# Four cosine channels in one stacked product, and PSUM pools divided at two stage starts, in a hybrid Fourier and convolution block

## The chip, the core and the metric

The kernel runs on one core of one Trainium2 chip. The metric is the device time of one execution in microseconds (us); of several executions the median counts. Times inside a run are read from one execution that the hardware profiler recorded, and are counted from the start of its span.

## What is computed

One encoder block over 1040 positions (16 meta tokens and 1024 inputs) of width 1024, all in float32. Cut to what matters here:

```
h     = rmsnorm(h_res)
u_a, c_g, b_g, v_b, gate_logits = split(h @ w_in)
y_a   = fourier_mix(u_a) @ w_fourier          # real part of fft2 over positions and the
                                              # 128 channels of each of 4 groups
y_b   = (b_g * dwconv(c_g * v_b)) @ w_conv_out
g0,g1 = sigmoid(gate_logits + b_gates)
h_res = h_res + rmsnorm((g0 * y_a + g1 * y_b) @ w_out)
up    = dwconv(rmsnorm(h_res) @ w_up);  a, v = split(up)
out   = h_res + rmsnorm((gelu(a) * v) @ w_down)
```

## The kernel before

**Products.** Each float32 operand is split into a high and a low part (`split`, lines 127 and 128: ACT casts the high part, DVE subtracts it to get the low one), and each product is made of three matmuls (`mm3`, lines 159, 161, 163: high x high, low x high, high x low). The large projections go through pairs of blocks with seven products each; the accumulators of such a pair are called a, b, c, d, of 514 or 512 columns each, and `B_c` and `up_c` are the last to be computed of the last pair before the Fourier stage and before the down projection. DVE (`B_s`, `up_1x`, line 144) adds them to others when PE has finished them.

**Fourier stage.** The real part of the 2-D transform needs, by symmetry, 65 cosine and 63 sine channels of each group of 128. `transformed` multiplies w_u by the channel transform while the projections run, and two ACT copies (line 612) put its result in the order: 260 cosine columns (4 groups of 65), then 252 sine columns (4 groups of 63). `fold` folds the positions, and both go to DRAM (`fold_d`). `next_fold(kt)` loads one of eight pieces `u` back (777 KB), and splits it. `u_mm(kt)` (line 731) makes 30 matmuls per kt, for five row blocks i of 105 or 101 positions, into five accumulators `pq0` to `pq4`. When kt = 7 is done, the accumulators are split into `pqh` and `pql`, and `dft` multiplies them by tables of cosines and sines (`cosh`, `cosl`, `sinh`, `sinl`, split from `cosr` and `sinr`, which are loaded inside this stage behind the splits of u4 and u5, whose memory they take over).

The cosine channels, 260 of them, are handled as three tiles `MA` of 87, 87 and 86 rows, the sine channels, 252, as two tiles `MB` of 126. `dft` writes them transposed and split: `ath`, `atl`, `bth`, `btl`.

**Merge.** For each of eight column blocks f of 128: `merge_operands(f)` loads the Fourier weights (`wfa`, `wfb`: the rows of channel k and of its mirror, which DVE adds or subtracts), the convolution weights and the gates. PE makes `yp` (cosine part: three tiles x three matmuls x two position chunks of 262 and 260 columns = 18 matmuls), `yq` (sine part, 12), and `yb` (convolution part, 36). DVE combines them: `y` from yp and yq, `s <- s, y`, then `s <- yb, s`. From f = 5 on, `out_weights` also loads and splits a block of w_out (`wor`, `wo`). `project(0)` follows.

**Later.** The gated MLP's up projection runs in pairs, and the down projection (products `dna` and `dnb` of 12 matmuls per k, operands `gd` and `wd`) in seven steps over 11 k.

**What sets the order.** Each engine runs its own list of instructions in order; the list follows the program with moves by a scheduler, and waits are by semaphore on what an instruction depends on. SP issues nearly all DMAs, in order. In PSUM there are eight banks. Each stage opens a pool of eight banks, and tiles get banks in the order of allocation; a tile waits until the last reader of the tile that had its bank is done. In before, `pq0` gets bank 0, that of `B_c`'s first half, and the first of `dna` bank 0, that of `up_c`.

Of the kernel before, what the change touches and what calls it, by code (L numbers as in the profile page):

```python
# [24 lines left out]
G = 4  # L25
# [25 lines left out]
HP = H + 1  # L51
Q = L // 4 + 1
NCH = [(0, 262), (262, 260)]
LT = 105
NLT = 5
# [4 lines left out]
FW = 2 * H  # L60
KC, KS = 65, 63
NA, NB = G * KC, G * KS
MA = [(0, 87), (87, 87), (174, 86)]
MB = [(0, 126), (126, 126)]


# [18 lines left out]

@with_exitstack
def block_kernel(ctx, tc, xT, w_u, w_in, w_fa, w_fa2, w_fb, w_fb2, w_co, w_out, w_up, w_dn,
                 par, dch, cos_t, sin_t, outT):
# [30 lines left out]
    V, S, SP = nc.vector, nc.scalar, nc.sync  # L119
# [4 lines left out]
    def split(hi, lo, src, scale=None, eng=V, copy=S.copy):  # L124

        if scale is None:
            a = copy(hi, src)  # L127
            b = eng.tensor_tensor(out=lo, in0=src, in1=hi.bitcast(F32), op=ALU.subtract)
# [14 lines left out]
    def add(out, a, b, eng=V):  # L143
        return eng.tensor_tensor(out=out, in0=a, in1=b, op=ALU.add).ins  # L144
# [101 lines left out]
    ring = Ring()  # L246
# [355 lines left out]
    def transformed(kt):  # L602

        r = ring.raw(f"wu{kt}")
        SP.dma_start(r[:, :512], w_u[kt])
        wp = wtile(psum, f"wp{kt}")[:, :512]
        for g in range(G):
            nc.tensor.matmul(wp[:, g * P : (g + 1) * P], r[:, g * P : (g + 1) * P], dc, start=True, stop=True)
        src = wp.rearrange("p (g k) -> p g k", k=P)
        t = r[:, 512:]  # L610
        for s, at, k in ((src[:, :, :KC], slice(0, NA), KC), (src[:, :, KC:], slice(NA, 512), KS)):
            S.copy(t[:, at].rearrange("p (g k) -> p g k", k=k), s)
        SP.dma_start(fold_d[kt, :, FW:], t)

    def fold(kt):
# [45 lines left out]


    mix_s = ExitStack()
    psum_s, psum = scope("psum2", 8, space=PSUM)

    COS_ROOMS = ("t2h", "t2l")
    SIN_ROOMS = ("t3h", "t4h")
# [7 lines left out]
    def merge_operands(f):  # L675
        s = room(S_ROOMS[f % 3], F32, f"s{f}")
        s0, s1 = s[:, :NT], s[:, NT : 2 * NT]
        ra, rb = ring.raw(f"wfa{f}"), ring.raw(f"wfb{f}")
        SP.dma_start(ra[:87, :384], w_fa[f])
        SP.dma_start(ra[:87, 384:768], w_fa2[f])  # L680
# [5 lines left out]
        add(ra[:87, :384], ra[:87, :384], ra[:87, 384:768])  # L686
        sub(rb[:126, :256], rb[:126, 256:512], rb[:126, :256])
        into = [None] * 3
        if f == 0:
            a, b = room("t1l", F32R, "w0a"), room("t4l", F32R, "w0b")  # L690
            into = [(a[:, :384], a[:, 384:768]), (a[:, 768:1024], a[:, 1024:1280]), (b[:, :512], b[:, 512:1024])]
        return s0, s1, [
            ring.piece(f"w{i}_{f}", src, p, t)
            for i, src, p, t in zip("abc", (ra[:87, :384], rb[:126, :256], rb[:, 512:]), (87, 126, P), into)
        ]

    def gated_conv():
# [9 lines left out]
            parts.append((hi, lo))  # L707
        return list(zip(*parts))

    def bank(name):  # L710
        return psum.tile([P, 512], F32, tag="bank", name=name)

    tp_ = new_pool(mix_s, "trans")
    ath, atl = (tp_.tile([P, 3, HP], F32R, name=n) for n in ("ath", "atl"))
    bth, btl = (tp_.tile([P, 2, HP], F32R, name=n) for n in ("bth", "btl"))

    with ExitStack() as st:
        fp = new_pool(st, "four", side="right")
        pqh, pql = (fp.tile([P, NLT, 512], F32R, name=n) for n in ("pqh", "pql"))
        acc = [bank(f"pq{i}") for i in range(NLT)]  # L720

        def u_mm(kt, xs, wc):
            (ch, cl), (sh, sl) = xs
            wh, wl = wc
            for i in range(NLT):
                n, s = _lrows(i), slice(i * LT, i * LT + _lrows(i))
                oa, ob = acc[i][:n, :NA], acc[i][:n, NA:]

                for o, (xh, xl), ks in ((oa, (ch, cl), slice(0, NA)), (ob, (sh, sl), slice(NA, 512))):
                    for n_, (a, b) in enumerate(((xh, wh), (xh, wl), (xl, wh))):  # L730
                        nc.tensor.matmul(  # L731
                            o, a[:, s], b[:, ks], start=kt == n_ == ks.start == 0, stop=kt == KT - 1 and n_ == 2,
                            skip_group_check=True,
                        )

        def table(tab, name, at):
            raw = room(at, F32, f"{name}r")[:LT, :TW]
            return raw, SP.dma_start(raw, tab).ins

        def table_parts(raw, name, at):  # L740
            parts = [room(n, F32R, f"{name}{i}")[:LT, :TW] for n, i in zip(at, "hl")]
            split(*parts, raw)
            return parts

        next_fold(4)
        for kt in range(KT):
            u_mm(kt, *folded[kt])
            if kt + 5 < KT:
                next_fold(kt + 5)
            if kt == 2:  # L750
                cos_r, _ = table(cos_t, "cos", "b11h")
                sin_r, last = table(sin_t, "sin", "t1l")
        cos_p = table_parts(cos_r, "cos", COS_ROOMS)
        sin_p = table_parts(sin_r, "sin", SIN_ROOMS)
        for i in range(NLT):
            n = _lrows(i)
            done = split(pqh[:n, i, :], pql[:n, i, :], acc[i][:n, :])

        def dft(tab, x, y, ms):
            (xh, xl), (yh, yl) = x, y  # L760
            name = f"dft{len(ms)}"
            at = 0
            for c, (a, w) in enumerate(NCH):
                outs = [bank(f"{name}_{m}_{c}") for m in range(len(ms))]
                for i in KINDS[c]:
                    n = _lrows(i)
                    th, tl = (t[:n, at : at + w] for t in tab)
                    at += w
                    for m, (m0, mw) in enumerate(ms):
                        mm3(  # L770
                            [outs[m][:mw, :w]],
                            (xh[:n, i, m0 : m0 + mw], xl[:n, i, m0 : m0 + mw]),
                            ([th], [tl]),
                            i == KINDS[c][0],
                            i == KINDS[c][-1],
                        )
                for m, (_, mw) in enumerate(ms):
                    split(yh[:mw, m, a : a + w], yl[:mw, m, a : a + w], outs[m][:mw, :w])

        dft(cos_p, (pqh[:, :, :NA], pql[:, :, :NA]), (ath, atl), MA)  # L780
        with behind(last, *done):
            merge_ins = [merge_operands(0)]
            ybs = gated_conv()
        dft(sin_p, (pqh[:, :, NA:], pql[:, :, NA:]), (bth, btl), MB)
    keep_s.close()
    ring.open(mix_s, "mergew", 7)
    op = new_pool(out_s, "proj", side="right")
# [17 lines left out]
    m0 = []  # L805
    for f in range(KT):
# [6 lines left out]
        yp = [bank(f"yp{f}_{c}") for c in range(2)]  # L813
        yq = [bank(f"yq{f}_{c}") for c in range(2)]
        for ps, w, (zh, zl), ms in ((yp, wa, (ath, atl), MA), (yq, wb, (bth, btl), MB)):
            for m, (_, mw) in enumerate(ms):
                mm3(
                    [o[:, :n] for o, (_, n) in zip(ps, NCH)],
                    tuple(t[:mw, m * P : (m + 1) * P] for t in w),
                    ([zh[:mw, m, a : a + n] for a, n in NCH], [zl[:mw, m, a : a + n] for a, n in NCH]),  # L820
                    m == 0,
                    m == len(ms) - 1,
                )
        for c, (a, n) in enumerate(NCH):
# [421 lines left out]

    dn_s, psum = scope("psum5", 8, space=PSUM)
    fn = new_pool(dn_s, "fin")  # L1250
    places = [f"{n}{i}" for n in ("b11", "t4", "t2", "t3", "b21", "b22", "t1") for i in "hl"]
    pairs_ = [r[:, i * 1024 : (i + 1) * 1024] for r in (room(t, F32, f"wd_{t}") for t in places[:NK]) for i in range(2)]
# [246 lines left out]
```

## Time and profile before

| | us |
|---|---|
| Median of 3 runs | 1219.29 |
| Lowest and highest | 1216.8, 1221.27 |
| The profiled execution | 1222.5 |
| Its span | 1220.7 |
| PE busy in the span | 1186.2 (97%) |
| DVE busy | 1001.6 (82%) |
| ACT busy | 550.6 (45%) |
| POOL busy | 0.4 (6 instructions) |
| TensorE clock, mean | 0.986 of full |

The stages by the trace: the projections up to 312.7; the Fourier stage's `pq` 314.85 to 345.1 and `dft` up to 356.1; the merge up to about 432; then w_out, the norms, and the up projection up to 989.0; the down projection from 991.9. In a row of the timeline stand the start, the time, the engine, the line, the operation, output and inputs, the shape, and in brackets how long the engine had been idle before and what it waited for. "x2" sums up two instructions. A row of the windows gives a stretch, the busy time of PE, PEld, DVE, ACT and POOL with the count of instructions, the clock granted to TensorE, the DMA engines' busy share and GB/s.

### The profile page before, as it was taken

What the parts mean: (1) busy time and instruction counts of PE and PEld (TensorE: products, weight loads), DVE (VectorE), ACT (ScalarE), POOL (GpSimd) and SP (SyncE); (2) the same over time, 40 slices, a digit from 0 to 9 for tenths busy, and PEclk for the clock granted to TensorE, in tenths of its full rate; (3) what the DMA queues carried; (4) which work ended last, traced back from release to release, by engine and by line L of the source; (5) the groups of instructions that cost most, each with busy time, mean ns of one, the idle gap of its engine ahead of it and who ended that gap; (6) DMA issues with size and microseconds to landing.
All of it is one profiled execution on the core that took longest, in us unless ns stands there. A gap on an engine that the chain in (4) does not pass through costs nothing.

```text
span 1220.7 us, 22312 instructions
## 1 busy us (share of the span) xinstructions
PE 1186.2 (97%) x8822; PEld 1143.0 (94%) x8822; DVE 1001.6 (82%) x1755; ACT 550.6 (45%) x999; POOL 0.4 (0%) x6
## 2 busy tenths in 40 slices
PE   8999999999999999998999999999999999999995
PEld 7999999999999999998999999999999988888884
DVE  8999876757488866989699999989988989766678
ACT  6743333323342344656545443444344434454562
POOL 0000000000000000000000000000000000000000
PEclk9999999999999999999999999999999999999998
DMA  6336554132876757465233334323222498354433
GB/s 248 122 111 219 196 174 165 61 130 85 258 226 216 250 168 116 127 112 152 96 120 123 112 132 147 122 96 130 96 78 87 146 318 313 95 164 121 132 128 138
DMA packets 78472, 184.01 MB, mean 151 GB/s; under 512 B 7934, under 2 KB 24910, under 8 KB 78368
## 3 DMA queue, kind: packets, MB, share of 16 engines
q1 hardware_dynamic: 78224, 182.47, 47.5%
q8 instruction: 69, 1.13, 0.4%
q14 instruction: 35, 0.29, 0.1%
q10 hardware_dynamic: 144, 0.12, 0.0%
HBM read 131.30 MB, written 51.26 MB: 150 GB/s over the span
## 4 chain that ended last, share of the span: by engine, by line
PE 75%; DVE 14%; DMA 7%; issue 2%; ACT 2%; SPq 0%; DVEq 0%; ACTq 0%
PE up_d L159 3%; PE up_d L163 3%; PE up_d L161 3%; PE up_c L161 3%; PE up_c L159 3%; PE dna L159 3%; PE up_c L163 3%; PE dna L161 3%; PE dna L163 3%; PE up_a L159 3%; PE up_a L163 3%; PE up_a L161 3%; PE pq L731 2%; PE dnb L163 2%; PE dnb L161 2%; PE dnb L159 2%
## 5 line engine op out<-in xcount | busy, mean ns | idle before, releaser
L159 PE MATMUL mo<-mh,wo 128*128 128x258 f32 (+1 forms) x256 | 73.9, 289 | 0.0
L163 PE MATMUL mo<-mh,wo 128*128 128x258 f32 (+1 forms) x256 | 73.1, 285 | 0.0
L161 PE MATMUL mo<-ml,wo 128*128 128x258 f32 (+1 forms) x256 | 72.9, 285 | 0.0
L159 PEld LDWEIGHTS mo<-mh,wo 128*128 128x128 f32 x256 | 49.3, 192 | 0.2
L161 PEld LDWEIGHTS mo<-ml,wo 128*128 128x128 f32 x256 | 49.2, 192 | 0.2
L163 PEld LDWEIGHTS mo<-mh,wo 128*128 128x128 f32 x256 | 49.2, 192 | 0.0
L127 ACT CAST up_1h<-up_1t 128x512 fp32r<-128x512 f32 x11 | 6.8, 622 | 75.2 <-DVE up_1t L144 52.5
L1096 ACT ACTIVATE up_1o<-up_1x,pr 128x512 f32<-128x512 f32 x33 | 26.9, 816 | 27.9 <-DVE up_1x L144 27.5
L1100 ACT ACTIVATE up_0o<-up_0o 128x512 f32<-128x512 f32 x44 | 27.8, 631 | 24.1 <-DVE up_0o L1098 23.8
L159 PE MATMUL up_d<-b22h,up_5h 128*128 128x258 f32 (+1 forms) x168 | 34.0, 283 | 0.8 <-DVE up_1x L144 0.8
L163 PE MATMUL up_d<-b22h,up_5l 128*128 128x258 f32 (+1 forms) x168 | 34.2, 284 | 0.0
L161 PE MATMUL up_c<-t3l,up_3h 128*128 128x258 f32 (+1 forms) x168 | 34.1, 285 | 0.0
L163 PE MATMUL up_b<-t2h,up_2l 128*128 128x258 f32 (+1 forms) x168 | 34.0, 283 | 0.0
L161 PE MATMUL up_d<-b22l,up_5h 128*128 128x258 f32 (+1 forms) x168 | 33.9, 283 | 0.0
L161 PE MATMUL up_b<-t2l,up_2h 128*128 128x258 f32 (+1 forms) x168 | 33.9, 283 | 0.0
L159 PE MATMUL up_c<-t3h,up_3h 128*128 128x258 f32 (+1 forms) x168 | 33.8, 282 | 0.0
L159 PE MATMUL up_b<-t2h,up_2h 128*128 128x258 f32 (+1 forms) x168 | 33.8, 282 | 0.0
L159 PE MATMUL up_c<-t4h,up_6h 128*128 128x258 f32 (+1 forms) x168 | 33.8, 282 | 0.0
L159 PE MATMUL up_d<-t1h,up_1h 128*128 128x258 f32 (+1 forms) x168 | 33.7, 282 | 0.0
L163 PE MATMUL up_d<-t1h,up_1l 128*128 128x258 f32 (+1 forms) x168 | 33.7, 282 | 0.0
L163 PE MATMUL up_c<-t3h,up_3l 128*128 128x258 f32 (+1 forms) x168 | 33.6, 281 | 0.0
L161 PE MATMUL up_d<-t1l,up_1h 128*128 128x258 f32 (+1 forms) x168 | 33.6, 281 | 0.0
(1321 smaller groups left out, 4328.4 us busy)
## 6 DMA issues: line engine op xcount, KB each, us to landing
g<-gp_d SPq DMA_DIRECT2D x35, 512.0 KB
up_1r<-in_w_up_dram SPq DMA_DIRECT2D x22, 512.0 KB
gp_d<-up_0o SPq DMA_DIRECT2D x44, 256.0 KB
up_0r<-in_w_up_dram SPq DMA_DIRECT2D x20, 512.0 KB
s<-sig_d SPq DMA_DIRECT2D x16, 514.0 KB
sig_d<-g_s SPq DMA_DIRECT2D x30, 257.0 KB
u<-fold_d SPq DMA_DIRECT2D x8, 777.0 KB
fold_d<-fold SPq DMA_DIRECT2D x8, 521.0 KB
```

The costliest lines, as they stand in the source:

```text
L127: a = copy(hi, src)
L159: nc.tensor.matmul(o, wh, h, start=first, stop=False, **kw)
L161: nc.tensor.matmul(o, wh, l, start=False, stop=False, **kw)
L163: newest[:] = [nc.tensor.matmul(o, wl, h, start=False, stop=last, **kw).ins]
L731: nc.tensor.matmul(o, a[:, s], b[:, ks], start=kt == n_ == ks.start == 0, stop=kt == KT - 1 and n_ == 2, skip_group_check=True,)
L1096: S.activation(t, ap[:, 1 : 1 + HALF], AF.Identity, bias=col("cb_ffn", b), scale=w(1))
L1100: S.activation(t, t, AF.Gelu_apprx_tanh)
```

## The change

**The stacked product.** Cosine channel 64 of each group, four in all, is taken out of the tiles. The other 4x64 = 256 fill two tiles of 128. The four go through the cosine `dft` as a third tile of 68 columns, `stacked`, that holds them three times, at columns 0, 32 and 64 (`AT`), zeros between. POOL fills it: two memsets ahead, then three copies of 105x4 after each high and each low part of the five accumulators, thirty in all. The result, 68 rows, is split into one tile `alone`: high part in rows 0 to 3 and 32 to 35, low part in rows 64 to 67. Its weights `w_alone` are loaded once as `wfl` (68x1024): high, low, high in the same rows. One matmul of 68 rows per chunk then gives all three terms, so `yp` is 2 + 12 matmuls for each f rather than 18; the `dft` has as many as before. `transformed` makes three copies rather than two, and `wfa` has 128x256 rather than 87x384 values.

**The banks.** In the Fourier scope the pool is divided into two banks (`late_banks`: outputs of `dft` that come later) and six, from which `pq0` to `pq4` take banks 2, 7, 6, 5, 4; the merge has a scope of its own with eight. In the down projection the pool is divided into 2, 4 and 2: `dna` gets banks 2 to 5, `dnb` 0, 1, 6, 7. The new waits by the program: `pq0` waits for DVE's read of an earlier accumulator (`t1_0`), `dna0` for PE's products, `dna1` for DVE's second read of `up_a`.

The diff, cut to its core:

```
-MA = [(0, 87), (87, 87), (174, 86)]
+MA = [(0, 128), (128, 128)]
+AT = [0, 32, 64]
+NS = AT[-1] + G
...
-        for s, at, k in ((src[:, :, :KC], slice(0, NA), KC), (src[:, :, KC:], slice(NA, 512), KS)):
-            S.copy(t[:, at].rearrange("p (g k) -> p g k", k=k), s)
+        for k0, k, at in ((0, KC - 1, 0), (KC - 1, 1, NA - G), (KC, KS, NA)):
+            S.copy(t[:, at : at + G * k].rearrange("p (g k) -> p g k", k=k), src[:, :, k0 : k0 + k])
...
-    psum_s, psum = scope("psum2", 8, space=PSUM)
+    psum_s, late_banks = scope("psum2", 2, space=PSUM)
+    psum = new_pool(psum_s, "psum2b", 6, space=PSUM)
...
+        stacked = [fp.tile([P, NLT, NS], F32R, name=f"stacked{n}") for n in "hl"]
+        for t in stacked:
+            nc.gpsimd.memset(t.bitcast(F32), 0.0)
...
+                r = ring.raw("wfl")
+                SP.dma_start(r[:NS, :], w_fl)
...
             done = split(pqh[:n, i, :], pql[:n, i, :], acc[i][:n, :])
+            for t, pq in zip(stacked, (pqh, pql)):
+                src = pq[:n, i, NA - G : NA].bitcast(F32)
+                for at in AT:
+                    nc.gpsimd.tensor_copy(t[:n, i, at : at + G], src)
+        w0, w1 = w_alone[:NS, :], w_alone[AT[1] : AT[1] + G, :]
+        S.copy(w0, r[:NS, :])
+        V.tensor_tensor(out=w1, in0=r[AT[1] : AT[1] + G, :], in1=w1.bitcast(F32), op=ALU.subtract)
...
+                        S.copy(alone[:NS, a : a + w], outs[m][:NS, :w])
+                        V.tensor_tensor(out=t, in0=outs[m][rest, :w], in1=t.bitcast(F32), op=ALU.subtract)
...
-        dft(cos_p, (pqh[:, :, :NA], pql[:, :, :NA]), (ath, atl), MA)
+        dft(cos_p, (pqh, pql), (ath, atl), [*MA, (None, NS)])
...
+    psum_s.close()
+    psum_s, psum = scope("psum2m", 8, space=PSUM)
...
+            if ps is yp:
+                for o, (a, n) in zip(yp, NCH):
+                    nc.tensor.matmul(
+                        o[:, :n], w_alone[:NS, f * P : (f + 1) * P], alone[:NS, a : a + n], start=True, stop=False
+                    )
...
-    dn_s, psum = scope("psum5", 8, space=PSUM)
+    dn_s, psum = scope("psum5", 2, space=PSUM)
+    firsts_, seconds = (new_pool(dn_s, f"psum5{n}", b, space=PSUM) for n, b in (("a", 4), ("b", 2)))
...
-    B, A = ([bank(f"dn{n}{f}") for f in range(4)] for n in "ba")
+    A = [bank(f"dna{f}", firsts_) for f in range(4)]
+    B = [bank(f"dnb{f}", None if f < 2 else seconds) for f in range(4)]
```

The instructions also move on two engines. On DVE, around the start of the Fourier stage, these rows stood in before (`t1_1` is the last work of the projections, `u42` and `u52` are low parts of u4 and u5):

```order
L144 TENSOR_TENSOR B1_s21_3735<-B1_c_3610,B1_u_3532 128x514
L150 TENSOR_TENSOR t1_1_3492<-B1_s21_3735,t1_1_3492 128x514
L128 TENSOR_TENSOR u42_3765<-u40_3763,u41_3764 128x1554
L128 TENSOR_TENSOR u52_3801<-u50_3799,u51_3800 128x1554
L128 TENSOR_TENSOR cosl_4032<-cosr_3877,cosh_4031 105x1566
```

Now the same place reads:

```order
L148 TENSOR_TENSOR B1_s21_3743<-B1_c_3617,B1_u_3539 128x514
L154 TENSOR_TENSOR t1_1_3499<-B1_s21_3743,t1_1_3499 128x514
L777 TENSOR_TENSOR w_alone_3763<-wfl_3898,w_alone_3763 4x1024
L132 TENSOR_TENSOR u42_3782<-u40_3780,u41_3781 128x1554
L132 TENSOR_TENSOR u52_3818<-u50_3816,u51_3817 128x1554
```

The weights' subtraction has come in ahead of u4's low part; ACT's cast for it stands ahead of u4's cast in the same way. The order of the table casts against those of u6 and u7 is as it was. At the end of the merge, for the last but one f, DVE had in before:

```order
L128 TENSOR_TENSOR wo1_5029<-wor1_5027,wo1_5029 128x1024
L150 TENSOR_TENSOR s6_4792<-s6_4792,y6_4936 128x1028
L128 TENSOR_TENSOR wo2_5125<-wor2_5123,wo2_5125 128x1024
L150 TENSOR_TENSOR s6_4792<-yb6_0_4978,s6_4792 128x344
L150 TENSOR_TENSOR s6_4792<-yb6_1_4979,s6_4792 128x342
L144 TENSOR_TENSOR s6_4792<-s6_4792 128x344
```

and has now:

```order
L154 TENSOR_TENSOR s6_4828<-s6_4828,y6_4968 128x1028
L154 TENSOR_TENSOR s6_4828<-yb6_0_5006,s6_4828 128x344
L154 TENSOR_TENSOR s6_4828<-yb6_1_5007,s6_4828 128x342
L148 TENSOR_TENSOR s6_4828<-s6_4828 128x344
L154 TENSOR_TENSOR s6_4828<-yb6_2_5008,s6_4828 128x342
L132 TENSOR_TENSOR wo2_5149<-wor2_5147,wo2_5149 128x1024
```

The third block's split (`wo2`) has moved behind the reads of yb6; `wo1` stands ahead of them in both.

More of the change, by code (lines that the diff above doesn't have):

```diff
@@ L87, in block_kernel @@
 def block_kernel(ctx, tc, xT, w_u, w_in, w_fa, w_fa2, w_fb, w_fb2, w_co, w_out, w_up, w_dn,
-                 par, dch, cos_t, sin_t, outT):
+                 w_fl, par, dch, cos_t, sin_t, outT):
     nc = tc.nc
@@ L678, in merge_operands @@
         ra, rb = ring.raw(f"wfa{f}"), ring.raw(f"wfb{f}")
-        SP.dma_start(ra[:87, :384], w_fa[f])
-        SP.dma_start(ra[:87, 384:768], w_fa2[f])
+        SP.dma_start(ra[:, :256], w_fa[f])
+        SP.dma_start(ra[:, 256:512], w_fa2[f])
         SP.dma_start(rb[:126, :256], w_fb[f])
@@ L685, in merge_operands @@
         SP.dma_start(s1, sig_d[:, KT + f, :])
-        add(ra[:87, :384], ra[:87, :384], ra[:87, 384:768])
+        add(ra[:, :256], ra[:, :256], ra[:, 256:512])
         sub(rb[:126, :256], rb[:126, 256:512], rb[:126, :256])
@@ L690, in merge_operands @@
             a, b = room("t1l", F32R, "w0a"), room("t4l", F32R, "w0b")
-            into = [(a[:, :384], a[:, 384:768]), (a[:, 768:1024], a[:, 1024:1280]), (b[:, :512], b[:, 512:1024])]
+            into = [(a[:, :256], a[:, 256:512]), (a[:, 512:768], a[:, 768:1024]), (b[:, :512], b[:, 512:1024])]
         return s0, s1, [
             ring.piece(f"w{i}_{f}", src, p, t)
-            for i, src, p, t in zip("abc", (ra[:87, :384], rb[:126, :256], rb[:, 512:]), (87, 126, P), into)
+            for i, src, p, t in zip("abc", (ra[:, :256], rb[:126, :256], rb[:, 512:]), (P, 126, P), into)
         ]
@@ L708, in gated_conv, with bank @@
         return list(zip(*parts))
-    def bank(name):
-        return psum.tile([P, 512], F32, tag="bank", name=name)
+    def bank(name, pool=None):
+        return (pool or psum).tile([P, 512], F32, tag="bank", name=name)
     tp_ = new_pool(mix_s, "trans")
-    ath, atl = (tp_.tile([P, 3, HP], F32R, name=n) for n in ("ath", "atl"))
+    ath, atl = (tp_.tile([P, 2, HP], F32R, name=n) for n in ("ath", "atl"))
+    alone = tp_.tile([P, HP], F32R, name="alone")
+    w_alone = tp_.tile([P, D], F32R, name="w_alone")
     bth, btl = (tp_.tile([P, 2, HP], F32R, name=n) for n in ("bth", "btl"))
@@ L763, in dft @@
             for c, (a, w) in enumerate(NCH):
-                outs = [bank(f"{name}_{m}_{c}") for m in range(len(ms))]
+                outs = [bank(f"{name}_{m}_{c}", late_banks if m < 2 and c == 0 else None) for m in range(len(ms))]
                 for i in KINDS[c]:
@@ L771, in dft @@
                             [outs[m][:mw, :w]],
-                            (xh[:n, i, m0 : m0 + mw], xl[:n, i, m0 : m0 + mw]),
+                            [t[:n, i, :] if m0 is None else t[:n, i, m0 : m0 + mw]
+                             for t in (stacked if m0 is None else (xh, xl))],
                             ([th], [tl]),
@@ L776, in dft @@
                         )
-                for m, (_, mw) in enumerate(ms):
-                    split(yh[:mw, m, a : a + w], yl[:mw, m, a : a + w], outs[m][:mw, :w])
-        dft(cos_p, (pqh[:, :, :NA], pql[:, :, :NA]), (ath, atl), MA)
+                for m, (m0, mw) in enumerate(ms):
+                    if m0 is None:
+                        rest = slice(AT[2], NS)
+                        t = alone[rest, a : a + w]
+                        S.copy(alone[:NS, a : a + w], outs[m][:NS, :w])
+                        V.tensor_tensor(out=t, in0=outs[m][rest, :w], in1=t.bitcast(F32), op=ALU.subtract)
+                    else:
+                        split(yh[:mw, m, a : a + w], yl[:mw, m, a : a + w], outs[m][:mw, :w])
+        dft(cos_p, (pqh, pql), (ath, atl), [*MA, (None, NS)])
         with behind(last, *done):
@@ L820, in block_kernel @@
                     ([zh[:mw, m, a : a + n] for a, n in NCH], [zl[:mw, m, a : a + n] for a, n in NCH]),
-                    m == 0,
+                    m == 0 and ps is yq,
                     m == len(ms) - 1,
@@ L1444 @@
     wf = a["w_fourier"][0].reshape(G, P, D)
-    k = np.arange(KC)
-    ra = wf[:, k].reshape(G * KC, D)
+    k = np.arange(KC - 1)
+    ra = wf[:, k].reshape(2 * P, D)
     ra2 = wf[:, (P - k) % P]
-    ra2[:, [0, KC - 1]] = 0
-    ra2 = ra2.reshape(G * KC, D)
+    ra2[:, 0] = 0
+    ra2 = ra2.reshape(2 * P, D)
+    w_fl = np.zeros((NS, D), np.float32)
+    for at in AT:
+        w_fl[at : at + G] = wf[:, KC - 1]
     rb = wf[:, 1 : KS + 1].reshape(G * KS, D)
@@ L1474 @@
         "w_in": _blocks(a["w_in"][0], 32),
-        "w_fa": rows(ra, MA, 87),
-        "w_fa2": rows(ra2, MA, 87),
+        "w_fa": rows(ra, MA, P),
+        "w_fa2": rows(ra2, MA, P),
         "w_fb": rows(rb, MB, 126),
@@ L1482 @@
         "w_dn": np.ascontiguousarray(a["w_down"][0].reshape(NF, P, D)),
+        "w_fl": w_fl,
         "par": np.ascontiguousarray(par),
```

## Prediction

> **What bounds the kernel now.** I read the waits of TensorE first, since the page has PE busy for 97% of the span. Two of the long ones lie where the change works, and a third, short one stands at the end of the merge. The columns are the total wait, how many, and the longest, in us.
>
> ```profile
> PE pq L731 <- DVE B_s L144: 2.1, 1, 2.1
> PE yb L159 <- DVE s L150: 0.8, 1, 0.8
> PE dna L159 <- DVE up_1x L144: 2.7, 1, 2.7
> ```
>
> The first wait stands before the Fourier stage, the third before the down projection: their first products need a bank whose last reader on DVE comes late. Next I read the stretches behind these waits; the columns to watch are the last three: PEclk, DMA share, GB/s.
>
> ```profile
> 315.00:317.00 2.00, 2.00 (x15) 2.00 (x15) 1.49 (x2) 0.91 (x1) 0.00 (x0) 0.76 1.02 190
> 317.00:319.00 2.00, 2.00 (x11) 2.00 (x11) 0.72 (x1) 0.00 (x0) 0.00 (x0) 0.50 0.86 332
> 319.00:321.00 2.00, 2.00 (x17) 2.00 (x16) 0.00 (x0) 0.63 (x1) 0.00 (x0) 0.88 1.02 402
> ...
> 410.00:420.00 10.00, 10.00 (x72) 10.00 (x71) 8.91 (x17) 2.88 (x7) 0.00 (x0) 1.00 0.90 273
> 420.00:428.00 8.00, 7.17 (x51) 6.69 (x50) 5.73 (x8) 3.06 (x5) 0.00 (x0) 1.00 0.72 236
> ...
> 992.00:994.00 2.00, 2.00 (x5) 1.61 (x6) 2.00 (x4) 0.63 (x1) 0.00 (x0) 0.50 0.83 299
> 994.00:996.00 2.00, 2.00 (x7) 1.58 (x7) 2.00 (x4) 0.00 (x0) 0.00 (x0) 0.67 1.00 324
> ```
>
> After each of the two long waits PE ran at half its clock for a while. The clock lost is 0.24x2 + 0.50x2 + 0.12x2 = 1.7 us after the wait of 2.1, and 0.50x2 + 0.33x2 = 1.7 us after that of 2.7. The short wait of 0.8 left the clock at 1.00. So a long wait costs its length and 1.7 us more. The Trainium skill, page "TensorE: Matmul & The Clock Gate", section "Why this matters for your kernels", asks only that idle gaps stay below about 3 us; by that rule gaps of 2.1 and 2.7 cost no clock. These rows contradict that, and the rows decide; the sum by the rule stands with the rivals.
>
> **Fourier stage: the wait moves.** The new bank of pq0 has a reader that is through early, so PE can go on when B_c ends. Four rows of PE give before's times; the rows of ACT and DVE under them are what feeds its seventh and eighth step.
>
> ```profile
> 312.33 0.40 PE L163 MATMUL B_c<-t4h,B_6l 128*128 128x258 f32 x2
> 314.85 0.34 PE L731 MATMUL pq<-u 128*105 128x260 f32 x1 [2.13 <-DVE B_s L144]
> 337.95 0.28 PE L731 MATMUL pq<-u 128*105 128x260 f32 x1
> 341.56 0.28 PE L731 MATMUL pq<-u 128*105 128x260 f32 x1
> ```
>
> ```profile
> 330.69 1.50 ACT L127 CAST cosh<-cosr 105x1566 fp32r<-105x1566 f32 x1 [8.83 <-DMA cosr<-in_cos_dram]
> 332.90 1.51 ACT L127 CAST sinh<-sinr 105x1566 fp32r<-105x1566 f32 x1 [0.71 <-DMA sinr<-in_sin_dram]
> 334.31 2.88 ACT L127 CAST u<-u 128x1554 fp32r<-128x1554 f32 x2
> ...
> 315.95 1.78 DVE L128 TENSOR_TENSOR u<-u,u 128x1554 fp32r<-128x1554 f32 x1 [0.51 <-ACT u L127]
> 335.83 1.78 DVE L128 TENSOR_TENSOR u<-u,u 128x1554 fp32r<-128x1554 f32 x1 [1.81 <-ACT u L127]
> 339.35 1.77 DVE L128 TENSOR_TENSOR u<-u,u 128x1554 fp32r<-128x1554 f32 x1
> ```
>
> One step kt takes 341.56 - 337.95 = 3.61 us at full clock. From 312.75 on, and without the half clock, the seventh step (kt 6) is due at 312.75 + 6x3.61 = 334.4. But the high part of u6 is ready at 335.8 and the low part at 335.83 + 1.78 = 337.6: ACT makes the high part only after the casts of the cosine and sine tables, and those wait for DMAs. The DMA share in the window rows is 0.86 to 1.02 there; PE does not set when these loads land. So the stage is bound by u6, and the idle time reappears in front of kt 6 in two pieces, 334.4 to 335.8 and, two products later, to 337.6, together some 3.0 us. Kt 6 then goes on at 337.7 where before it began at 337.95: a gain of 0.25. Whether this broken gap also halves the clock, no row shows. It is nearest to the waits of 2.1 and 2.7 and far above the harmless 0.8, so I take the full 1.7. Kt 7 finds u7 ready (339.35 + 1.77 = 341.1, due 341.3). The stage ends **1.4 us later** (between 0.25 earlier and 1.7 later).
>
> The preparation of w_alone lies in the same place. Its DVE instruction, 4x1024, is put ahead of u4's low part; the row of 1024 elements further down took 1.22. DVE had been idle for 0.51 before u4, so u4's low part, and with it the issue of the cosine load behind it on SP, comes 0.7 us later. PE needs u4 only at 312.75 + 4x3.61 = 327.2 and finds it ready at 318.4. The cosine load may land 0.7 us later; then cosh ends at 332.9, when sinh began anyway. So I cost it at nothing; without that cover it costs 0.7. The cast of w_alone on ACT, the load of its 278 KB (68x1024x4 bytes), the eight additional tiny copies on ACT and the splits of alone, which stand for those of ath's third tile, lie beside busy PE time: nothing.
>
> **The copies on POOL.** Thirty copies of 105x4 fill the stacked tiles, after each split of pq. The widest of POOL's six rows in before is a memset of 128x128; the first stacked input exists when ACT's first cast below ends, and the last is read by the last cosine product.
>
> ```profile
> 0.73 0.20 POOL L113 MEMSET ones<- 128x128 f32 x1 [0.29 <-POOLq L1488]
> ...
> 342.47 3.45 ACT L127 CAST pqh<-pq 105x512 fp32r<-105x512 f32 x5 [5.28 <-PE pq L731]
> ...
> 351.58 0.28 PE L163 MATMUL dft<-cosh,pql 101*86 101x260 f32 x1
> ```
>
> A far neighbour is a narrow DVE operation, from the groups by form (busy us, mean ns):
>
> ```profile
> L128 DVE TENSOR_TENSOR wb_7l<-wfb,wb_7h 126x256 fp32r<-126x256 f32 x1 | 0.4, 417 | 0.0
> ```
>
> Five casts in 3.45 us make the first end near 343.15, so all thirty have 351.6 - 343.15 = 8.4 us, or 0.28 us each, before PE waits. The copies lie between next to nothing and 0.42 (DVE's, 64 times wider). I take 0.20, POOL's own row, and no wait; at 0.42 it would be 30x0.42 - 8.4 = 4.2 us.
>
> **Merge.** PE's rows of the last f give the price of the products that go; the rows of ACT and DVE give what holds its end.
>
> ```profile
> 421.42 0.41 PE L159 MATMUL yp<-ath,wa_7h 87*128 87x262 f32 x2
> 423.62 0.41 PE L159 MATMUL yq<-bth,wb_7h 126*128 126x262 f32 x2
> 426.22 0.84 PE L159 MATMUL yb<-yb_t3l,wc_7h 128*128 128x342 f32 x2 [0.83 <-DVE s L150]
> ```
>
> ```profile
> 421.15 1.06 ACT L127 CAST wo<-wor 128x1024 fp32r<-128x1024 f32 x1 [2.89 <-DMA wor<-in_w_out_dram]
> ...
> 422.24 1.22 DVE L128 TENSOR_TENSOR wo<-wor,wo 128x1024 fp32r<-128x1024 f32 x1 [2.25 <-ACT wo L127]
> 423.38 1.22 DVE L150 TENSOR_TENSOR s<-s,y 128x1028 f32<-128x1028 f32 x1
> 424.52 1.22 DVE L128 TENSOR_TENSOR wo<-wor,wo 128x1024 fp32r<-128x1024 f32 x1
> 425.66 0.93 DVE L150 TENSOR_TENSOR s<-yb,s 128x344 f32<-128x344 f32 x2
> ```
>
> Eighteen yp products took 423.62 - 421.42 = 2.20 us, 0.122 each, and the yq rows with 126 in place of 87 rows run at the same pitch; so the stacked product with 68 costs 0.122 too. Four fewer for each of eight f are 32x0.122 = **3.9 us less** work. Not all of it arrives. The last f's second yb product waits for DVE's read of yb6, which stands behind wo1's split, and that waits for a DMA (2.89 of idle time on ACT, DMA share 0.90). PE was there at 426.22 - 0.83 = 425.4 and will be at 425.4 + 1.4 - 3.9 = 422.9. DVE's second wo split now stands behind the read, so the read moves by 425.66 - 424.52 = 1.14 even if the load lands as before: PE goes on at 426.2 - 1.1 = 425.1. If the load came earlier by all of PE's 2.5 us, it would go on at once. SP issues it when its slot is freed, which moves with PE, but the queue is nearly full; I take half, 1.25. PE goes on near 423.8, after a wait of 0.9 that costs no clock. So after Fourier stage and merge **2.4 us** are gained together. The ends: 3.3 gained without a wait; with no earlier landing 1.1 gained and a wait of 2.2, which by the rows above loses 1.7 again: 0.6 lost.
>
> **Down projection.**
>
> ```profile
> 988.79 0.40 PE L163 MATMUL up_c<-t4h,up_6l 128*128 128x258 f32 x2
> 991.93 0.76 PE L159 MATMUL dna<-gd_0h,wd_0h 128*128 128x512 f32 x1 [2.73 <-DVE up_1x L144]
> 999.05 0.39 PE L159 MATMUL dna<-gd_2h,wd_2h 128*128 128x512 f32 x1
> 1001.77 0.39 PE L159 MATMUL dna<-gd_3h,wd_3h 128*128 128x512 f32 x1
> ...
> 996.36 0.62 ACT L127 CAST gd_3h<-g 128x512 fp32r<-128x512 f32 x1 [3.73 <-PE dna L161]
> ...
> 987.18 0.75 DVE L1098 SCALAR_TENSOR_TENSOR up_1o<-up_a,pr,up_1o 128x512 f32<-128x512 f32 x1
> 991.10 0.69 DVE L144 TENSOR_TENSOR up_1x<-up_c,up_u 128x514 f32<-128x514 f32 x1
> 997.01 0.69 DVE L128 TENSOR_TENSOR gd_3l<-g,gd_3h 128x512 fp32r<-128x512 f32 x1 [0.89 <-ACT gd_3h L127]
> ```
>
> Dna0 waited for the read of up_c (991.10 + 0.69). Now its bank is up_b's, free long before, and dna1's was read by up_a's last reader, done at 987.93. PE can begin at about 989.07, 2.86 us earlier, and without the gap the half clock goes too: 2.86 + 1.7 = 4.5 us. What comes late next is gd_3l, the first operand not ready by 990; one k takes 1001.77 - 999.05 = 2.72 us, so k = 3 needs it at 989.07 + 3x2.72 = 997.2, its low part 0.2 later. It ended at 997.7, but ACT's cast ahead of it waited for products of dna (3.73), which come 4.5 us earlier; DVE, idle for 0.89 before gd_3l, can then end it at about 996.8. So **4.5 us** less, between 2.8 (the half clock stays) and 4.6.
>
> **Sum.** 2.4 + 4.5 = 6.9 us. The profiled execution took 1222.5 us (span 1220.7), 3.2 above the median of 1219.3; it would take 1215.6, and the median 1212.4.
>
> **Rivals.** *All of it arrives*: the tables land early enough that u6 holds nothing up, and wor lands in time. For it: the landings are read from one execution, and a busy queue may sort itself otherwise. Against it: 337.6 is set by DMAs and by ACT's order, not by PE. At most 2.1 + 1.7 + 3.9 + 0.8 + 4.5 = 13 us, at least 9: 1206 to 1210. (If only the clock survives the broken gap at kt 6, PE comes to f = 7 at 421.2, half of that 4.2 moves the load, and PE goes on at 423.0: 3.2 + 4.5 = 7.7, within my forecast.)
>
> *The half clock is not the gap's*: the first products of a new stage run at half clock whatever comes before, and gaps cost none. Then the Fourier stage gains 0.25 (its slow start is covered by the 3 us to spare before kt 6), the merge's end comes 3.2 earlier as just worked out, and dna gains its 2.9 of idle time: 6.1, 1213.2. The row with 1.00 behind a short gap and those with 0.50 behind both long ones speak against it. The Trainium skill's page "TensorE: Matmul & The Clock Gate", which allows no loss for such gaps, would come out there too.
>
> *The merge's end gives its gain back*: wor lands as before, 0.6 lost there, 3.9 left in all: 1215.4. With dna also slowed by an operand, 2: 1217.
>
> *POOL decides* (the other side): each copy waits for a semaphore and takes more than 0.28 us; the first cosine product of the stacked tile then waits, in every i. From 0.51 us each (30x0.51 - 8.4 = 6.9) the kernel is no faster, at 0.72 it is 6.3 slower: 1225.6. Against it: POOL's row of 0.20 for 32 times the width. The Trainium skill, page "GPSIMD Engine Reference", section "Performance versus the Vector engine", has elementwise work there 1.96 times as long as on DVE, for wide tensors. An estimate from it: DVE's rows of 1024 and 256 elements give 0.15 us for 4, so 0.30 on POOL, and a wait of 0.6 us; no row of before shows it.
>
> *It doesn't do what it says*: a bank of pq or dna still has a late reader, and one gap stays: 4.5 lost of the gain at worst, 1217.
>
> **How the numbers follow.** A measurement of this kernel tells about 0.5%, 6.1 us, from no change. My forecast (5 to 9 us gained) 58%; all of it arrives 10%; half clock not the gap's 8%; merge gives it back 10%; POOL 9%, of which 4 beyond 6.1 us slower; a bank stays late 3%; 2% for a collision that I do not see. The forecast lies only 0.8 beyond the 0.5% line, so two thirds of its 58 count as faster, and half of the 8: 39 + 10 + 4 = 53%. Slower by over 0.5%: 4 from POOL and the 2, 6%. Within: 41%. The range leaves out the far ends: 1207 (12.3 gained) to 1217.5 (1.8 gained).
>
> **What would show it.** Right: no wait at 312.7 and 989.0, PEclk 1.00 in the first 4 us of the down projection; PE waiting for ACT and DVE u at kt 6, with 0.50 behind it; twelve yp products and two of w_alone in each f, 1.71 us; a yb wait of about 0.9 at f = 7; POOL copies at about 0.2. Wrong: no gap at kt 6, or PE waiting for POOL in the cosine products, or dna waiting for gd.

## Result, and the profile after

The changed kernel takes 1209.53 us (median of 5 runs, 1204.0 to 1212.61) against 1219.29 for the kernel before (5 runs, 1215.72 to 1221.76): ratio 0.9922, 95% interval 0.9897 to 0.9947. That is 9.8 us less, where 6.9 were forecast. In a second series of runs, beside four of the experiments, it took 1202.38 against 1212.92: ratio 0.9911, interval 0.9892 to 0.9930.

The waits of TensorE in the profile after, for 300 to 360 us (total, how many, the longest):

```profile
PE pq L742 <- DVE u L132: 1.4, 1, 1.4
PE pq L742 <- ACT u L131: 0.2, 1, 0.2
```

The wait of 2.1 ahead of pq is gone and a shorter one, in two pieces, stands at kt 6. Two pieces were forecast there, but 3.0 us of them; the rows of PE further down have 0.24 and 1.45. For the down projection the same question (975 to 1000 us) has no row at all. The clock of TensorE (third column from the right) stays whole at both places:

```profile
334.00:336.00 2.00, 0.65 (x5) 0.65 (x6) 1.97 (x2) 0.88 (x1) 0.00 (x0) 1.00 0.97 345
336.00:338.00 2.00, 2.00 (x19) 2.00 (x18) 2.00 (x2) 0.00 (x0) 0.00 (x0) 1.00 0.99 356
...
978.00:980.00 2.00, 2.00 (x16) 1.87 (x15) 1.97 (x4) 0.67 (x2) 0.00 (x0) 1.00 0.97 369
980.00:982.00 2.00, 2.00 (x11) 1.63 (x10) 2.00 (x4) 0.89 (x2) 0.00 (x0) 1.00 0.83 330
```

What feeds kt 6, and kt 6 itself, in the timelines of ACT, DVE and PE:

```profile
327.89 1.50 ACT L131 CAST cosh<-cosr 105x1566 fp32r<-105x1566 f32 x1 [7.43 <-DMA cosr<-in_cos_dram]
330.60 1.50 ACT L131 CAST sinh<-sinr 105x1566 fp32r<-105x1566 f32 x1 [1.20 <-DMA sinr<-in_sin_dram]
332.00 2.87 ACT L131 CAST u<-u 128x1554 fp32r<-128x1554 f32 x2
...
333.52 1.78 DVE L132 TENSOR_TENSOR u<-u,u 128x1554 fp32r<-128x1554 f32 x1 [2.30 <-ACT u L131]
...
333.54 0.37 PE L742 MATMUL pq<-u 128*105 128x260 f32 x1 [0.24 <-ACT u L131]
335.35 0.48 PE L742 MATMUL pq<-u,u 128*105 128x260 f32 x2 [1.45 <-DVE u L132]
```

ACT still makes u6 behind both table casts, but the tables landed early. B_c ends at 311.75 here and at 312.72 in before; counted from there u6's low part was ready after 23.5 us, not 24.9.

The cast of the w_out block that the last f of the merge waited for in before:

```profile
413.19 1.05 ACT L131 CAST wo<-wor 128x1024 fp32r<-128x1024 f32 x1 [1.39 <-DMA wor<-in_w_out_dram]
```

The group of the stacked products (the shortest, the middle and the longest in ns, then the first and the last start in us), and under it four of the copies on POOL:

```profile
L847 PE MATMUL yp<-alone,w_alone x16: 280/286/397, 353.6 to 415.7; 68*128 68x262 f32 x8, 68*128 68x260 f32 x8
```

```profile
340.53 0.44 POOL L774 CAST stackedh<-pqh 105x4 fp32r<-105x4 f32 x3 [19.47 <-ACT pqh L131]
...
343.44 2.77 POOL L774 CAST stackedl<-pql 105x4 fp32r<-105x4 f32 x3
346.16 1.54 POOL L774 CAST stackedh<-pqh 101x4 fp32r<-101x4 f32 x3
347.63 0.42 POOL L774 CAST stackedl<-pql 101x4 fp32r<-101x4 f32 x3
```

The wo block that before's ACT could cast only 0.3 us ahead of the last f's products (421.15, yp 421.42) is now there 2.35 ahead of them (413.19, yp 415.54), and no wait of yb is left. Three copies of POOL take 0.44 us where nothing disturbs them.

Where the time went, by the first and last products of the stages in the two profiled executions (us):

| from, to | before | after | difference | forecast |
|---|---|---|---|---|
| end of B_c to first dft product | 32.42 | 30.73 | -1.7 | +1.4 |
| dft | 10.97 | 11.16 | +0.2 | 0 |
| first yp to first product with w_out | 76.00 | 70.73 | -5.3 | -3.8 (both: -2.4) |
| w_out, norms, up projection | 557.08 | 554.93 | -2.2 | 0 |
| end of up_c to end of dna | 216.63 | 212.07 | -4.6 | -4.5 |

These two executions lie 14.2 us apart in their spans, more than the medians (9.8): before's lay above its median (1222.5 against 1219.3), after's below (1208.31 against 1209.5). The row from w_out to the up projection, where PE's products are the same, shows what else differs between executions: before's trace has three stretches of half clock there, after's two.

### The profile page after: what moved, and what is told of

Same layout as the page of the kernel before. It is cut to its first block, busy times and chain, and to the rows that moved or that the text cites. A ratio compares the mean times of both kernels' runs of the same rounds, so it can differ in the third digit from the quotient of the medians.

```text
span 1206.5 us, 22298 instructions
## 1 busy us (share of the span) xinstructions
PE 1177.1 (98%) x8790; PEld 1134.4 (94%) x8790; DVE 1000.9 (83%) x1756; ACT 552.0 (46%) x1008; POOL 8.4 (1%) x38
## 4 chain that ended last, share of the span: by engine, by line
PE 81%; DVE 12%; DMA 4%; ACT 1%; issue 1%; SPq 0%; DVEq 0%; ACTq 0%
PE up_d L167 3%; PE up_c L165 3%; PE up_c L163 3%; PE up_d L163 3%; PE up_d L165 3%; PE up_c L167 3%; PE up_a L163 3%; PE up_a L167 3%; PE up_a L165 3%; PE dna L163 3%; PE dna L165 3%; PE dna L167 3%; PE dnb L165 2%; PE dnb L163 2%; PE dnb L167 2%; PE up_b L167 2%
## 5 line engine op out<-in xcount | busy, mean ns | idle before, releaser
L1134 ACT ACTIVATE up_0o<-up_0o 128x512 f32<-128x512 f32 x44 | 27.8, 631 | 23.5 <-DVE up_0o L1132 23.3
```

What stands on the lines that cost most here:

```text
L1134: S.activation(t, t, AF.Gelu_apprx_tanh)
```

## Experiments

The ratios are against the kernel before on the same chip.

**One part alone.** First the down projection's pool alone:

```
-    dn_s, psum = scope("psum5", 8, space=PSUM)
+    dn_s, psum = scope("psum5", 2, space=PSUM)
+    firsts_, seconds = (new_pool(dn_s, f"psum5{n}", b, space=PSUM) for n, b in (("a", 4), ("b", 2)))
...
-    B, A = ([bank(f"dn{n}{f}") for f in range(4)] for n in "ba")
+    A = [bank(f"dna{f}", firsts_) for f in range(4)]
+    B = [bank(f"dnb{f}", None if f < 2 else seconds) for f in range(4)]
```

> Only the division of the PSUM pool at the down projection is taken over; everything ahead of it is as before. Theory A (a wait costs its own length, and half a clock window more if more than half of one window of 3.41 us is idle): no wait in front of dna, no half clock behind it, 2.9 + 1.7 = 4.5 us less, 1214.8 us. Rival B (a new stage starts at half clock whatever comes before it): 2.9 us less, 1216.4 us, and a PEclk of about 0.5 in the first 3 us of dna.

Measured: ratio 0.9988 (0.9971 to 1.0005), 1212.73 against 1214.36 us. Its profile has no wait ahead of dna, no half clock, and 212.07 us from the end of up_c to the end of dna, the same as after. So rival B's sign, half a clock in the first 3 us of dna, is not there, and the stage gains its 4.6 us in the trace. But the medians show only 1.6 us, at most 3.5 by the interval, so theory A's 4.5 is not borne out as the gain of the whole kernel. Part of the gap may be that before does not pay its half clock in every execution (see the clock below); then the gain lies between 2.9 and 4.6, and its lower part fits the interval. There is one trace of each kernel, so this is not shown and stays open.

Then the Fourier stage's pool alone, with the merge's own scope:

```
-    psum_s, psum = scope("psum2", 8, space=PSUM)
+    psum_s, late_banks = scope("psum2", 2, space=PSUM)
+    psum = new_pool(psum_s, "psum2b", 6, space=PSUM)
...
+    psum_s.close()
+    psum_s, psum = scope("psum2m", 8, space=PSUM)
```

> Only the division of the PSUM pool at the Fourier stage is taken over (with the merge's own scope); three tiles of cosine channels as before. Theory A: the wait ahead of pq (2.1 us and 1.7 us of half clock) goes, and what is left of it stands ahead of kt 6, as long as u6's splits behind the table casts make it, 1.5 to 3 us; the stage ends 0.3 to 2 us earlier, and the merge's end, which waits for a DMA, may keep or lose that: 1217.5 to 1219.5 us. The prediction on record: the stage ends 1.4 us later, 1220.7 us. Rival C (all of it arrives): no wait at kt 6, 3.8 us less, 1215.5 us.

Measured: 0.9998 (0.9985 to 1.0010). The waits of PE:

```profile
PE dna L159 <- DVE up_1x L144: 2.8, 1, 2.8
...
PE pq L732 <- DVE u L128: 1.4, 1, 1.4
PE pq L732 <- ACT u L127: 0.7, 1, 0.7
```

The first dft product starts 32.7 us behind the end of B_c (before: 32.4): the wait of 2.1 has come back as 0.7 and 1.4 at kt 6, and here with the half clock. This is the prediction's mechanism, but not its size: the stage ends 0.3 us later, not 1.4. By the interval the kernel gains at most 1.8 us and loses at most 1.2, so theory A (nothing to 1.8 less) fits, rival C (3.8 less) falls, and the 1.4 more of the prediction lies just outside.

The stacked product alone, which is the change without the lines of these two diffs:

> Only the stacked product is taken over; the PSUM pools are as before. Theory A: 32 matmuls of 0.122 us fewer are 3.9 us, and the wait of 0.8 at the last f goes as well since the wo loads come earlier: 5.1 us less, 1214.2 us, with the waits of 2.1 before pq and of 1.3 to 2.7 before dna still there. The prediction on record: 3.9 us of work less, but the last f waits for the wo load, so 2.4 to 3.3 us less, 1216 to 1217 us. Rival D (the loads came early only because the Fourier stage began early): a wait of 1 us or more at the last f.

Measured: 0.9953 (0.9939 to 0.9967), 5.0 us less. Its waits of PE:

```profile
PE pq L741 <- DVE B_s L148: 2.2, 1, 2.2
...
PE dna L163 <- DVE up_1x L148: 1.3, 1, 1.3
```

No row for yb. From the first yp to the first product with w_out it takes 70.6 us, so theory A holds, and rival D falls: the wo loads come early without the Fourier stage's early start. The wait ahead of dna is 1.3 here and does not halve the clock.

Both diffs, no stacked product:

> Both divisions of the PSUM pools, no stacked product. Theory A: the parts add up: 4.5 from the down projection and 0 to 2 from the Fourier stage, 1212.8 to 1214.8 us. Rival E (the parts share a gain, as a start that comes earlier lets DVE lag further behind): less than 4 us, over 1215.3 us.

Measured: 0.9957 (0.9939 to 0.9974), 4.3 us less by the medians. That lies between theory A (4.5 to 6.5 less) and rival E (under 4), and the interval, 3.2 to 7.4, takes in both: not settled. The two divisions alone (0.9988 and 0.9998) multiply to 0.9986, so by the medians the parts come to less than the whole. The traces show one way in which executions differ: at kt 6 this one waited only 0.7 us, and dft began 29.6 us behind B_c, 3.1 sooner than in fourier_banks. Why the medians differ so is open.

**The changed kernel again, and without the first of the diffs above.**

> The changed kernel again, on the chip and beside the runs that the next three are compared with. All theories: 0.7 to 1% below before. Theory A (half clock after a window of 3.41 us with over 1.8 us idle): waits of 2.5 us ahead of ms_h and 2.6 us ahead of up_a halve the clock where one window holds nearly all of them, the wait of 1.4 us at kt 6 does not.

> The changed kernel with the down projection's pool undivided again. Theory A (the wait ahead of dna is as long as DVE lags, and DVE lags by how late w_down's first block lands): the wait is 1.3 us as in the run with the stacked product alone, too short for a half clock, and the kernel is 1.7 us slower than the changed one. The prediction on record: the wait is 2.7 us and halves the clock, 4.5 us slower.

Measured: 0.9911 (0.9892 to 0.9930), 1202.38 us, and 0.9925 (0.9908 to 0.9941), 1203.23 us. So on top of the other parts the down projection's banks are worth 0.9 us in the medians and 1.5 in the stage of the two traces; the two intervals overlap, so the 0.9 is not clear of nothing. Theory A's wait of 1.3 us without a half clock is there, the prediction's 2.7 is not. Waits of PE without them, then those of the changed kernel's second profile at kt 6 with the clock behind them:

```profile
PE dna L163 <- DVE up_1x L148: 1.3, 1, 1.3
```

```profile
334.69 0.37 PE L742 MATMUL pq<-u 128*105 128x260 f32 x1 [0.78 <-ACT u L131]
336.50 0.76 PE L742 MATMUL pq<-u,u 128*105 128x260 f32 x2 [1.45 <-DVE u L132]
```

```profile
336.00:338.00 2.00, 1.50 (x7) 1.50 (x8) 1.97 (x2) 0.03 (x1) 0.00 (x0) 0.57 0.85 292
338.00:340.00 2.00, 2.00 (x12) 2.00 (x11) 1.96 (x2) 0.00 (x0) 0.00 (x0) 0.58 0.88 345
```

The same kernel as in the profile after, but here u6 came later, the gap at kt 6 was 0.78 + 1.45, where the expectation had counted on 1.4, and the clock halved: dft starts 32.7 us behind B_c, 0.3 later than in before. The half clock that the prediction expected at kt 6, and its absence, are two executions of one kernel.

**When does the clock halve?** In every trace the changes of the granted clock lie on a raster of 3.41 us. I summed PE's idle time in each window of that raster, from 100 us to PE's last product, in 14 traces (before, after and the twelve experiments), for windows with over 0.3 us idle, and looked at the clock in the window behind:

```
idle time in the window     windows   clock in the next window
0.3 to 1.79 us                   95    1.00 in all
1.86 us (before)                  1    0.50
1.90 us (load_by_act)             1    1.00
1.95 to 3.18 us                  26    0.50 in all
```

So what counts is not a wait's length but how much of it falls into one window: over about 1.85 us, more than half of it. A window at half clock does half of its work later, which is the 1.7 us. A wait of 2.4 us that lay across a border (1.50 and 0.88, profile after, ahead of up_z) cost no clock; one of 1.86 within a window did. The rule is read off these rows; no run moved a wait across a border on purpose. The Trainium skill, page "TensorE: Matmul & The Clock Gate", section "What's actually happening", gives a free-running window of 3413 ns, and the raster agrees. Its table there has the half clock after at least one idle window; in these rows 1.95 us of idle time within a window was enough, and the rows decide.

**u6 ahead of the tables.** `next_fold` keeps the instructions of its split, and the table splits are queued behind those of u6 and u7:

```
+        with behind(*fold_splits[6]):
             cos_p = table_parts(cos_r, "cos", COS_ROOMS)
+        with behind(*fold_splits[7]):
             sin_p = table_parts(sin_r, "sin", SIN_ROOMS)
```

> The changed kernel with the table splits queued behind u6's (cosines) and u7's (sines) on ACT and DVE. The prediction's reason (u6 is held by ACT's order behind the table casts): no wait at kt 6, dft starts 1.9 us earlier, 1.9 us less than the changed kernel, unless POOL's copies, held up by DVE, then come too late for the stacked product (up to 1 us of wait). Rival F (u6 is held by its load): the wait at kt 6 stays, no change.

Measured: 0.9906 (0.9890 to 0.9923), 1201.55 us, its five runs within 1200.68 and 1202.13. PE has no wait from 300 to 360 us, and dft starts 28.6 us behind B_c. ACT's timeline shows why:

```profile
325.91 1.49 ACT L131 CAST u<-u 128x1554 fp32r<-128x1554 f32 x1 [6.04 <-PE pq L742]
327.30 1.50 ACT L131 CAST cosh<-cosr 105x1566 fp32r<-105x1566 f32 x1
329.49 1.50 ACT L131 CAST u<-u 128x1554 fp32r<-128x1554 f32 x1 [0.69 <-PE pq L742]
330.90 1.49 ACT L131 CAST sinh<-sinr 105x1566 fp32r<-105x1566 f32 x1
```

u6 is cast as soon as PE has left its place, 6 us earlier than in after; the cosine table comes no later for it, the sine table 0.3 us. So ACT's order, not u6's load, held kt 6: shown, and rival F falls. Against the changed kernel on the same chip the median is 0.8 us lower where 1.9 were expected (no interval was taken between the two), and the changed kernel's runs reach up to 1206.7.

The version with ms_h, a later product that waits for sums by DVE, moved as well:

```
+        if c == 2:
+            hooks[7] = hooks.pop(6)
```

> As the kernel before, and in addition the product of the squared sums ms_h of the second chunk is moved behind eight columns of 24 matmuls of project, so that PE has work while DVE sums up. Theory A: the wait of 2.5 us there goes, and the half clock behind it: 2.5 us, and up to 1.7 more, less than u6_before_tables, 3.4 on average. Rival G (the wait is part of a chain that ends later anyway): it shows up again ahead of up_z or up_a, and nothing is gained.

Measured: 0.9903 (0.9886 to 0.9919), 1201.12 us. The wait it was to remove was 2.5 us in the profile after but 0.7 in u6_before_tables, so there was little left to gain; the median is 0.4 us lower, and theory A and rival G are not told apart.

**POOL's copies made twice.**

```
                     nc.gpsimd.tensor_copy(t[:n, i, at : at + G], src)
+                    nc.gpsimd.tensor_copy(t[:n, i, at : at + G], src)
```

> As u6_before_tables, with each of POOL's thirty copies made twice. The copies take 0.12 us each, but in the profile after one of them lasted 2.5 us and one 1.3 us, while DVE ran operations with two inputs in SBUF. Theory J (POOL is held up by those DVE operations; what counts is how many copies are left when they begin): 30 more copies are 3.7 us more before the hold-up, so about fifteen of the sixty are left when DVE begins, PE waits for stackedl in the cosine products for 1 to 4 us, and half a clock window follows if one window holds over 1.8 us of it: 1 to 6 us slower than u6_before_tables. Rival (the prediction's formula, 8.4 us for all copies): 60x0.12 = 7.2 us, no wait, no change.

Measured: 0.9939 (0.9917 to 0.9960), against 0.9906 for u6_before_tables on another chip, some 4 us more. Its waits, and POOL's timeline:

```profile
PE dft L163 <- POOL stackedh L777: 2.2, 1, 2.2
PE dft L167 <- POOL stackedl L777: 0.5, 2, 0.3
```

```profile
341.05 0.43 POOL L777 CAST stackedl<-pql 105x4 fp32r<-105x4 f32 x3
341.42 2.75 POOL L776 CAST stackedh<-pqh 105x4 fp32r<-105x4 f32 x3
344.11 1.53 POOL L777 CAST stackedh<-pqh 105x4 fp32r<-105x4 f32 x3
345.59 0.43 POOL L776 CAST stackedl<-pql 105x4 fp32r<-105x4 f32 x3
```

Sixty copies of 0.12 us would have fitted the prediction's 8.4 us; PE waited all the same, 2.7 us, since two groups of three took 2.75 and 1.53 in place of 0.43. So theory J holds, and the prediction's formula does not. The slow spots lie where DVE runs operations with two inputs in SBUF. The Trainium skill, page "GPSIMD Engine Reference", section "Specifications", says that POOL shares its SBUF interfaces with DVE and names DVE's instructions with two SBUF inputs as a case of contention. The traces agree: in the profile after, one copy lasts from 343.44 to 345.97, and five such operations of DVE stand back to back from 343.90 to 345.93. In the nine traces with these copies 19 last over 1 us, and each ends 0.05 us or less after such an operation; beside `pql`, which DVE makes from one input in PSUM and one in SBUF, the copies keep their pace. That the long copy begins 0.46 us ahead of the first of the five is not explained.

**Eighteen yp matmuls again.** The base is u6_before_tables:

```
-            if ps is yp:
+            for n_ in range(3 if ps is yp else 0):
```

> As u6_before_tables, but the stacked product is made three times in every f (so its share is counted three times in the result), which gives yp the 18 matmuls of the kernel before. Theory K (matmuls are priced at 0.122 us, and the wo loads come early because of the other loads, not because of PE): 3.9 us slower than u6_before_tables, no wait of yb at the last f. Rival L (they come early because PE frees their places early): a wait of 0.8 us or more at the last f, 4.7 to 5.5 us slower.

Measured: 0.9922 (0.9897 to 0.9947). First yp to first product with w_out: 74.8 us against 70.7 in u6_before_tables, 4.1 us for 32 matmuls. (The medians give 1.9 us by the ratios on two chips, and 4.7 against load_by_act, further down, on the same chip.) There is no wait of yb; ACT casts the wo block at 412.95 and PE is at the last f's yp at 417.19:

```profile
412.95 1.05 ACT L131 CAST wo<-wor 128x1024 fp32r<-128x1024 f32 x1 [0.48 <-DMA wor<-in_w_out_dram]
...
417.19 0.91 PE L849 MATMUL yp<-alone,w_alone 68*128 68x262 f32 x6
```

So theory K holds and rival L falls: the load is 4.2 us early with as many matmuls as in before. SP's timeline of before and of this run shows what changed; the instructions are a load of convolution weights and the one of the gates next in SP's list:

```profile
380.30 0.38 SPq L683 DMA_DIRECT2D wfb<-in_w_co_dram  x1
382.34 0.35 SPq L684 DMA_DIRECT2D s<-sig_d  x1
```

```profile
375.91 0.37 SPq L689 DMA_DIRECT2D wfb<-in_w_co_dram  x1
376.38 0.38 SPq L690 DMA_DIRECT2D s<-sig_d  x1
```

In before SP stands still for 1.7 us there, until the store of an earlier result (`merged_d`, issued at 377.74) has landed; in yp_padded that store, issued at 373.45, has landed by 376.4. Before's SP has four such waits in the merge, yp_padded none:

```profile
SPq L684 <- DMA merged_d<-s: 8.0, 4, 3.3
```

The issue of the wor load itself, in before, after and yp_padded:

```profile
411.76 0.33 SPq L200 DMA_DIRECT2D wor<-in_w_out_dram  x1
406.05 0.33 SPq L204 DMA_DIRECT2D wor<-in_w_out_dram  x1
406.87 0.42 SPq L204 DMA_DIRECT2D wor<-in_w_out_dram  x1
```

Counted from the last f's first yp (421.42, 415.54, 417.19), it is issued 9.7, 9.5 and 10.3 us ahead: it goes when DVE has freed its slot, and that moves with PE. What differs is the time from its issue to ACT's cast, 9.4 us in before, 7.1 and 6.1 in the others. In the five traces without the stacked product it is 8.8 to 10.2 us, in the nine with it 6.1 to 8.1. A queue that is less crowded because SP issued the loads ahead of it sooner would do this, but it is not shown: whether wfa's new form (128 rows rather than 87), DVE's new order or something else lets these transfers land sooner was not taken apart.

**Why does dna wait 1.3 or 2.7?** ACT's wait for the first block of w_down was 3.6 us in before and 1.4 in after. Two kernels test whether wfl's load is behind it: before with it, and u6_before_tables with it on ACT's queue.

```
+                r = ring.raw("wfl")
+                SP.dma_start(r[:68, :], w_fl)
...
-                SP.dma_start(r[:NS, :], w_fl)
+                nc.scalar.dma_start(r[:NS, :], w_fl)
```

> The kernel before with one load of 68x1024 values more (unused), at the place where the change loads wfl, so that every later DMA takes the next of the eight completion semaphores in turn. In before and in the kernels without the stacked product the first block of w_down kept ACT waiting for 2.9 to 3.8 us and dna for 2.7 us; with it, for 1.4 to 1.6 and 1.3 us. Theory H (the turn of the semaphores decides when that block is issued and lands): ACT waits about 1.5 us and dna 1.3, without a half clock, 3 us less than before. Rival I (it comes with the merge's other loads or its end): 3.6 and 2.7 us as in before, no change in time.

> As u6_before_tables, but wfl is loaded by ACT's queue, so that SP's list is that of the kernel before. Theory H (a load more in SP's turn of semaphores): ACT waits 3.6 us for the first block of w_down again; dna does not wait, as its bank is read early, so the time is the same within 1 us. Rival I: ACT waits 1.4 us as with the load on SP.

Measured: extra_load 0.9993 (0.9975 to 1.0011), load_by_act 0.9884 (0.9863 to 0.9904), 1202.31 us against 1215.71, the best ratio of all; no run of the changed kernel stands beside it on that chip, and its interval overlaps that of u6_before_tables. The wait of ACT in each, and that of dna in the first:

```profile
ACT wd_0h L127 <- DMA wd_b11h<-in_w_dn_dram: 4.5, 1, 4.5
...
PE dna L159 <- DVE up_1x L144: 3.6, 1, 3.6
```

```profile
ACT wd_0h L131 <- DMA wd_b11h<-in_w_dn_dram: 1.5, 1, 1.5
```

Theory H falls both ways: the load added does not shorten the wait, the load taken off SP does not lengthen it. In the eight traces with 14 yp products for each f the wait is 1.3 to 1.6 us, in the six with 18, yp_padded with its 3.1 among them, 2.9 to 4.5. That is a regularity and no cause; the cause is open.

## Why the forecast was right, and where it was not

**The clock.** "So a long wait costs its length and 1.7 us more" was drawn from two waits, both of which lay within one window. The price is 1.7 us if more than about 1.85 us of the wait falls in one window, else nothing; the raster's position differs from run to run. At kt 6 the prediction took the full 1.7: paid in changed_again and fourier_banks, not in after, banks_only and without_down_banks.

**Fourier stage.** The mechanism was right: the wait moved to kt 6 in two pieces, u6's high and low part, behind the table casts. The size was off because 337.6 was taken as fixed: u6 was ready 1.3 us sooner in after, and 1.7 of clock were not paid, so the stage came 1.7 us earlier where 1.4 later was forecast. In changed_again it came 0.3 later. That the tables landed early in after is luck of the execution and no part of the forecast.

**Merge.** 32 matmuls were priced at 3.9 us; measured 4.1. The step that failed is the load: "SP issues it when its slot is freed, which moves with PE, but the queue is nearly full; I take half, 1.25". The issue did move with PE, but then the load took 7.1 us to ACT's cast and not 9.4. So it came 8.0 us earlier and PE 5.9, the wait at the last f went entirely, and the merge gave 5.3 us where 3.8 were forecast. With it goes that SP hardly stood still for the stores any more (0.6 us in after, 8.0 in before); that this is the cause is not shown.

**Down projection.** 4.5 forecast, 4.6 between the two traces. But in the presence of the stacked product dna's wait is 1.3 and leaves the clock alone, and the banks then give 0.9 us by the medians. The term counted a wait of before that is shorter in every trace with the stacked product and the old banks (1.3 in both), and why it is shorter is open.

**POOL.** 0.20 us a copy was forecast; in a row they follow each other every 0.12, and PE does not wait: right. But the 8.4 us that all copies were thought to have are less, since POOL loses some 3.4 us of them beside DVE's operations (2.77 and 1.54 in place of 0.44 each).

**Sum.** 6.9 us forecast, 9.8 and 10.5 measured in two series. Both lie above the 5 to 9 us of the main forecast and in the span of the rival "All of it arrives" (9 to 13), which had 10%. That rival is half true: wor landed in time, but u6 still held kt 6 up for 1.7 us in after and 2.2 in changed_again. Of the parts by the medians, the stacked product is worth 5.0 and both divisions together 4.3. The Fourier stage's division gives 0.2 us alone, but some 3.4 on top of the stacked product (0.9953 and 0.9925, on two chips); why is open. That the sum came near is in part luck: the merge was forecast too low and the down projection, with the stacked product in place, too high.

## What to carry to other kernels

Price a wait by where it ends, not by its length: the engine behind it in order, and what that engine waits for, decide what the removal of a wait uncovers, and here an order of two casts (u6 ahead of the tables) took away the wait that the banks had only moved. Where TensorE waits for 2 to 3 us, expect half a window of clock on top in some runs and not in others, and bring the wait below 1.8 us if it can't go. When two parts of a change act on one chain, price the second with the first in place.

## What the runs showed of the hardware

- The clock of TensorE halves for a raster window of 3.41 us if PE was idle for more than about 1.85 us of the window before it: of 123 windows with over 0.3 us of idle time, none of the 95 with up to 1.79 us led to half clock and all of the 26 from 1.95 us did; one at 1.86 did and one at 1.90 did not.
- Copies of 105x4 on POOL follow each other every 0.12 us, and one lasts up to 2.5 us where DVE runs operations with both inputs in SBUF (2.53 us beside five of them, 1.29 beside one of 1.22).
